# Gate and up products of a SwiGLU stage by seven block products instead of eight, on one Trainium2 core

## The chip, the cores and the metric

The kernel runs on 1 core of one Trainium2 chip. The core has a matrix engine (TensorE, PE in the profile; its weight loads are PEld), VectorE (DVE), ScalarE (ACT), GpSimd (POOL), a queue for transfers (SyncE, SP) and 16 DMA engines. The metric is the device time of one launch in microseconds; lower is better.

## The reference, cut to what matters

A decoder trunk of two layers on 512 tokens of 1024 features, all in float32. Each layer has a retention branch, an mLSTM branch, a gated merge with an output projection and a LayerNorm, and then the part that the change is about:

```python
gu = x @ w_gate_up[l]                                   # (512, 1024) @ (1024, 5632)
hidden = jax.nn.silu(gu[..., :D_FF]) * gu[..., D_FF:]   # D_FF = 2816
x = _layer_norm(DEEPNORM_ALPHA * x + hidden @ w_down[l], ln2_g[l], ln2_b[l])
```

## The kernel before, in words

**Products of split operands.** Every matrix product is made from operands split into a high part (rounded to the matrix engine's fast float32 format, `F32R`) and a low part (the rest). A product is the sum of three matmuls: high by high, high by low, low by high. The activations are held transposed, features on the 128 partitions, as a pair of tiles [128, 8 k-tiles, 512 tokens].

**The weight stream.** All weights lie in DRAM as units of [128, 1024] float32, in the order in which they are used (`layer_plan`, L48-90). An "F" unit holds 128 output columns for all 8 k-tiles; a "T" unit holds 512 columns of two k-tiles. For each unit SP issues a DMA of 512 KB into a raw tile (L133-139, `NRAW` = 3 raw tiles), ScalarE casts it to a high part `whi` (L147) and VectorE subtracts to make the low part `wlo` (L126, called from L154). `take` hands a prepared unit to the matmuls, `used` counts it off and prepares up to `LOOK` = 5 units ahead into a ring of `NRING` = 6 pairs. 

**Order of work.** The instructions of TensorE and SP stand in program order (`manual_schedule`, L100). Those of the other engines are placed by a scheduler of the framework, and each engine then works through its list in that order. Tiles with the same tag share a fixed number of buffers, and an instruction that writes a tile waits until the buffer's earlier tile is done with.

**Stages of a layer.** Retention, its gate and projection; mLSTM, its gate and projection; the output projection in two halves of 512 columns (`tok_units`, then `tok_blocks`, which holds four units over all four token blocks and ends each block with its LayerNorm, L722-738). `block_flip` (L740-751) transposes each normed block into the pair `x1h`, `x1l`: per half block one ScalarE cast (L750) and one VectorE subtraction.

**SwiGLU before.** For each of 22 tiles of 128 hidden features there is one gate unit and one up unit. Each is one `feat` (L194-199): 8 k-tiles times 3 matmuls of 128x128 weights by 512 tokens (L188-190) into one PSUM bank. The gate bank becomes SiLU on ScalarE (L816); the up bank is multiplied with it on VectorE (L824); the hidden tile is split at once, high on ScalarE (L825), low on VectorE (L126), into tiles that lie in buffers free by then. The first four units (hidden tiles 0 and 1) are done by `feat_split` (L214-224): the first 256 tokens of all four, between them the last two flips, then the other 256 tokens.

**Down stage before.** `tok_units` and `tok_blocks` over 22 hidden tiles, two per unit, twice (512 columns each, `DOWN0` and `DOWN1`, L44-45), with 128x128 blocks of the hidden tiles against 512 columns of weights (L247-249), and the residual and LayerNorm at the end.

Of the kernel before, what the change touches and what calls it, by code (L numbers as in the profile page):

```python
# [15 lines left out]
P = 128  # L16
# [14 lines left out]
# Columns of w_in.  # L31
# [13 lines left out]
DOWN1 = [(k, k + 1) for k in range(8, FT, 2)] + [(0, 1), (2, 3), (4, 5), (6, 7)]  # L45


def layer_plan():  # L48
    """Order of the weight units of a layer: ("F", matrix, column) holds 128 columns of all 8
    k-tiles, ("T", matrix, (k0, k1), column) holds 512 columns of two k-tiles."""  # L50
# [34 lines left out]
    for j in range(FT):  # L85
        feat("gu", j * P)
        feat("gu", DFF + j * P)
    tok("down", 0, DOWN0)
# [4 lines left out]
NUNIT = len(layer_plan())  # L93
UNIT_IF = layer_plan().index(("F", "if", 0))
# [3 lines left out]
def decoder_trunk(ctx: ExitStack, tc: tile.TileContext, wall, xT_in, x_in, pvec, lnp, rtab, out):  # L98
# [30 lines left out]
    total = L * NUNIT  # L129
    raw_t, prep_t = {}, {}  # L130
    state = {"dma": 0, "prep": 0, "used": 0, "next": 0}

    def issue_dma(n):  # L133
        while state["dma"] < min(n, total):
            i = state["dma"]
            r = wp.tile([P, UNIT], F32, tag="raw", name="wraw", bufs=NRAW)
            nc.sync.dma_start(r, wall[i])
            raw_t[i] = r
            state["dma"] += 1

    def prep_to(n):
        while state["prep"] < min(n, total, state["used"] + NRING):
            i = state["prep"]
            issue_dma(i + 1)
            r = raw_t.pop(i)
            hi = wp.tile([P, UNIT], F32R, tag="hi", name="whi")
            nc.scalar.copy(hi, r)  # L147
            lo = None
            if i % NUNIT == UNIT_IF:
# [51 lines left out]
    def feat_if(xh, xl, evac):  # L201
        """The gate columns are few: high parts in the first half of the columns, low ones in the second."""
# [11 lines left out]
    def feat_split(xh, xl, evacs, between):  # L214
        """The first units behind a norm: two token blocks first, the others when they are there."""
# [9 lines left out]

    def first_units(evacs):
        """The first units, in step with the loads of the activations."""
        ws = [take() for _ in evacs[:NRAW]]
# [11 lines left out]
        for ev in evacs[NRAW:]:  # L240
            feat(xh, xl, ev)
# [9 lines left out]
    def tok_units(pms, sh, sl, kts, first, last, evac=None):  # L251
        """Units of two k-tiles over all token blocks, one after the other."""
        for n, kk in enumerate(kts):
            w = take()
# [10 lines left out]
    def tok_blocks(pms, sh, sl, kts, first, evac, within):  # L265
        """Units of two k-tiles, one token block after the other."""
# [34 lines left out]
    for i in range(NRAW):  # L301
        firsts.append([wp.tile([P, UNIT], F32, tag="raw", name="wraw", bufs=NRAW),
                       wp.tile([P, UNIT], F32R, tag="hi", name="whi"), wp.tile([P, UNIT], F32R, tag="lo", name="wlo")])
# [18 lines left out]
    state["dma"] = state["prep"] = NRAW  # L322
    tab = reg.tile([P, 6, S], F32, tag="tab", name="rtab")
    nc.sync.dma_start(tab[:, 0:2], rtab[:, 0:2])
    issue_dma(NRAW + 1)
    nc.sync.dma_start(tab[:, 2:6], rtab[:, 2:6])
    issue_dma(2 * NRAW)
# [48 lines left out]
    def three(pa, a, b, first, last):  # L376
        """Product of two split operands without the product of their low parts."""
# [4 lines left out]
    def weighted(box, vh, vl, hh, nv, done):  # L382
        """Sums over s of weights and values, a token block at a time."""
# [59 lines left out]
    for l in range(L):  # L443
# [22 lines left out]
        # ---- mLSTM gates, by halves of the tokens: log sigmoid, its running sum b from the half's start,  # L466
        # a = i - b, M = max(m, running max a) with m the stabiliser at the half's start ----
# [254 lines left out]
        def block_norm(b, y, st, gb, dst):  # L722
            """LayerNorm of a token block."""
# [16 lines left out]
        def block_flip(b, y, nxt):  # L740
            """A token block transposed and split for the next products."""
            nh, nl = nxt
            for c in range(2):
# [7 lines left out]
                lo_of(nl[a], src, nh[a])  # L751

# [25 lines left out]
        ev0, ev1, within, between = norm_evacs(xr, gb, x1d, (x1h, x1l))  # L778
# [5 lines left out]
        hAh, hAl = bigpair(cur, f"h{l}")  # L784
        hid = {}
        for k in range(8):
            hid[k] = (hAh[:, k], hAl[:, k])

        def piece(tag, k0):
            t = reg.tile([P, 4, S], F32R, tag=tag, name=f"hd_{tag}")  # L790
            return t

        hp = {}

        def hidden(j):
            if j in hid:
                return hid[j]
            if j < 20:
                tags = {2: ("vh", "vl"), 3: ("gt", "qk"), 4: ("pp", "oo")}[j // 4]
                if tags not in hp:  # L800
                    hp[tags] = (piece(tags[0], j), piece(tags[1], j))
                a, c = hp[tags]
                hid[j] = (a[:, j % 4], c[:, j % 4])
            else:
                if "tab" not in hp:
                    hp["tab"] = piece("tab", j)
                a = hp["tab"]
                hid[j] = (a[:, (j - 20) * 2], a[:, (j - 20) * 2 + 1])
            return hid[j]
# [10 lines left out]
        def up_ev(j):  # L820
            def ev(pm):
                s = gates.pop(j)
                hh, hl = hidden(j)
                nc.vector.tensor_tensor(out=s, in0=s, in1=pm, op=ALU.mult)  # L824
                nc.scalar.copy(hh, s)  # L825
                lo_of(hl, s, hh)
            return ev

        feat_split(x1h, x1l, [gate_ev(0), up_ev(0), gate_ev(1), up_ev(1)], between)
        for j in range(2, FT):  # L830
            feat(x1h, x1l, gate_ev(j))
            feat(x1h, x1l, up_ev(j))

        xr = []
        for b in range(NB):
            t = scratch([P, DM], "xr2")
            nc.gpsimd.dma_start(t, x1d[b * P : (b + 1) * P, :])
            xr.append(t)
        hh_, hl_ = (lambda k: hid[k][0]), (lambda k: hid[k][1])
# [3 lines left out]
        else:  # L843
            nxt = bigpair(oth, f"x2{l}")
# [8 lines left out]
        tok_units([aux_bank() for _ in range(NB)], hh_, hl_, DOWN0, True, True, ev0)  # L853
        pms = [main_bank() for _ in range(NB)]
        tok_units(pms, hh_, hl_, DOWN1[:2], True, False)
        gb[0] = reg.tile([P, 2, DM], F32, tag="vh", name="gb2")
        nc.gpsimd.dma_start(gb[0], lnp[l, 2:4].unsqueeze(0).broadcast_to([P, 2, DM]))
        tok_units(pms, hh_, hl_, DOWN1[2:7], False, False)
        tok_blocks(pms, hh_, hl_, DOWN1[7:], False, ev1, within)
        if not last:  # L860
            xh, xl = nxt
# [5 lines left out]
def _layout(inputs):  # L867
# [32 lines left out]
    # Tables of the positions: rotary cosines and signed sines, decays of the four heads.  # L900
# [39 lines left out]
```

## Time and profile before

| what | value |
|---|---|
| time, median of 3 runs | 1830.61 us (1829.69 to 1831.13) |
| span of the profiled execution | 1828.3 us |
| the median over that span | 2.3 us more |
| instructions | 21351 |
| bytes moved by DMA | 200.71 MB, mean 110 GB/s |
| weight transfers from SP | 307 of 512 KB |
| mean granted TensorE clock | 0.997 of full speed |

The profiled execution is one of its own. Its time is given by its span, from the first to the last instruction; what lies around that is not in the profile. In the page, a row of a group ends with its busy time and the mean ns of one instruction, then the idle time of the engine before them and what ended it. Durations of matmuls overlap, so the rate of TensorE is read from the distance of their starts.

### The profile page before, as it was taken

The page shows a single profiled execution, that of the slowest core. Times are in us where ns is not written, and L with a number is a line of the kernel's source. Part 1 is how long each engine was busy: PE and PEld are TensorE (multiplying, and loading weights), DVE is VectorE, ACT ScalarE, POOL GpSimd, SP SyncE. Part 2 cuts the span into 40 slices and gives each one's busy share as a digit, 9 for nine tenths or more (in the row PEclk, how much of TensorE's full clock was granted, in tenths as well). Part 3 has the DMA queues.
Part 4 walks back from the last instruction along what each step waited for, and adds up shares of the span by engine and source line. Part 5 has one row for each costly group of instructions (what it writes and reads, how often), then busy time and mean ns, then how long its engine had stood idle before and what let it go on. Part 6 is the DMA issues. An engine that isn't in the chain of part 4 may idle for free.

```text
span 1828.3 us, 21351 instructions
## 1 busy us (share of the span) xinstructions
PE 1812.2 (99%) x8600; PEld 1518.3 (83%) x8600; DVE 874.2 (48%) x1406; ACT 644.4 (35%) x932; POOL 106.7 (6%) x145
## 2 busy tenths in 40 slices
PE   8999999999999999999999999999999999999998
PEld 7788888888889888888898888888888888888886
DVE  6665236654455333323476543467525643333234
ACT  4434326554313223221144343357432233222220
POOL 2020000010000000000120100010100100000000
PEclk9999999999999999999999999999999999999999
DMA  6222243234224232342432222422433332223321
GB/s 232 82 84 78 93 150 105 81 127 156 97 93 139 92 104 93 108 134 93 149 128 86 87 81 93 163 87 75 150 138 103 105 126 92 96 101 115 126 104 46
DMA packets 55011, 200.71 MB, mean 110 GB/s; under 512 B 6233, under 2 KB 8153, under 8 KB 52865
## 3 DMA queue, kind: packets, MB, share of 16 engines
q1 hardware_dynamic: 48528, 168.32, 27.5%
q0 software_dynamic: 6384, 31.04, 4.7%
q8 instruction: 67, 1.10, 0.3%
q14 instruction: 32, 0.25, 0.0%
HBM read 186.73 MB, written 12.60 MB: 109 GB/s over the span
## 4 chain that ended last, share of the span: by engine, by line
PE 96%; DVE 2%; ACT 1%; issue 1%; DMA 0%; SPq 0%; DVEq 0%; ACTq 0%
PE pm L190 18%; PE pm L188 18%; PE pm L189 18%; PE pm L247 9%; PE pm L249 9%; PE pm L248 9%; PE pa L248 3%; PE pa L247 3%; PE pa L249 3%; PE pa L378 1%; PE pa L379 1%; PE pa L380 1%; PE pa L433 1%; PE pa L352 1%; DVE wlo L126 1%
## 5 line engine op out<-in xcount | busy, mean ns | idle before, releaser
L126 DVE TENSOR_TENSOR wlo<-wraw,whi 128x1024 fp32r<-128x1024 f32 (+2 forms) x320 | 380.4, 1192 | 526.3 <-ACT whi L147 518.9
L147 ACT CAST whi<-wraw 128x1024 fp32r<-128x1024 f32 x307 | 322.9, 1052 | 859.8 <-PE pm L189 376.1
L188 PE MATMUL pm<-x11h,whi 128*128 128x512 f32 (+1 forms) x384 | 142.8, 372 | 0.0
L188 PE MATMUL pm<-x10h,whi 128*128 128x512 f32 (+1 forms) x384 | 142.8, 372 | 0.0
L189 PE MATMUL pm<-x10l,whi 128*128 128x512 f32 (+1 forms) x384 | 142.6, 371 | 0.0
L189 PE MATMUL pm<-x11l,whi 128*128 128x512 f32 (+1 forms) x384 | 142.6, 371 | 0.0
L190 PE MATMUL pm<-x10h,wlo 128*128 128x512 f32 (+1 forms) x384 | 142.6, 371 | 0.0
L190 PE MATMUL pm<-x11h,wlo 128*128 128x512 f32 (+1 forms) x384 | 142.6, 371 | 0.0
L188 PE MATMUL pm<-x20h,whi 128*128 128x512 f32 (+1 forms) x288 | 106.9, 371 | 0.0
L247 PE MATMUL pm<-whi,x0h 128*128 128x512 f32 x256 | 102.7, 401 | 3.3 <-DVE rvl L126 1.7
L190 PE MATMUL pm<-x20h,wlo 128*128 128x512 f32 (+1 forms) x288 | 105.4, 366 | 0.0
L189 PE MATMUL pm<-x20l,whi 128*128 128x512 f32 (+1 forms) x288 | 105.3, 366 | 0.0
L247 PE MATMUL pm<-whi,x20h 128*128 128x512 f32 x256 | 102.3, 400 | 0.6 <-DVE rvl L126 0.6
L249 PE MATMUL pm<-wlo,x0h 128*128 128x512 f32 x256 | 100.7, 393 | 0.0
L248 PE MATMUL pm<-whi,x0l 128*128 128x512 f32 x256 | 100.5, 393 | 0.0
L249 PE MATMUL pm<-wlo,x20h 128*128 128x512 f32 x256 | 100.3, 392 | 0.0
L248 PE MATMUL pm<-whi,x20l 128*128 128x512 f32 x256 | 100.0, 391 | 0.0
L824 DVE TENSOR_TENSOR sl<-sl,pm 128x512 f32<-128x512 f32 x44 | 30.3, 688 | 138.1 <-PE pm L190 138.1
L188 PE MATMUL pm<-x0h,whi 128*128 128x512 f32 x232 | 91.8, 396 | 0.0
L190 PE MATMUL pm<-x0h,wlo 128*128 128x512 f32 x232 | 90.4, 390 | 0.0
L189 PE MATMUL pm<-x0l,whi 128*128 128x512 f32 x232 | 90.3, 389 | 0.0
L188 PEld LDWEIGHTS pm<-x10h,whi 128*128 128x128 f32 x384 | 72.3, 188 | 12.6
(346 smaller groups left out, 3608.6 us busy)
## 6 DMA issues: line engine op xcount, KB each, us to landing
wraw<-wall SPq DMA_DIRECT2D x307, 512.0 KB, 3.3
yd<-sga POOLq DMA_DIRECT2D x4, 1024.0 KB, 5.0
ya<-yd POOLq DMA_DIRECT2D x4, 1024.0 KB, 6.1
gb<-lnp POOLq DMA_DIRECT2D x4, 1024.0 KB, 5.4
x1d<-xr POOLq DMA_DIRECT2D x8, 512.0 KB, 2.9
xr<-x1d POOLq DMA_DIRECT2D x8, 512.0 KB, 4.7
negm<-md POOLq DMA_DIRECT2D x2, 1026.0 KB, 6.7
xr<-xtok POOLq DMA_DIRECT2D x4, 512.0 KB, 3.9
```

What stands on the lines that cost most here:

```text
L126: nc.vector.tensor_tensor(out=out_lo, in0=full, in1=hi.bitcast(F32), op=ALU.subtract)
L147: nc.scalar.copy(hi, r)
L188: nc.tensor.matmul(pm[:, c0:c1], lhsT=hi[:, k], rhs=xh[:, k, c0:c1], start=(k == 0), stop=False)
L189: nc.tensor.matmul(pm[:, c0:c1], lhsT=hi[:, k], rhs=xl[:, k, c0:c1], start=False, stop=False)
L190: nc.tensor.matmul(pm[:, c0:c1], lhsT=lo[:, k], rhs=xh[:, k, c0:c1], start=False, stop=(k == KT - 1))
L247: nc.tensor.matmul(pm, lhsT=sh(k)[:, a], rhs=hi[:, j], start=first, stop=False)
L248: nc.tensor.matmul(pm, lhsT=sl(k)[:, a], rhs=hi[:, j], start=False, stop=False)
L249: nc.tensor.matmul(pm, lhsT=sh(k)[:, a], rhs=lo[:, j], start=False, stop=last)
L352: nc.tensor.matmul(pa[:, :HC], lhsT=k[:, t0:t1], rhs=q[:, t0:t2], start=True, stop=True)
L378: nc.tensor.matmul(pa, lhsT=a[0], rhs=b[0], start=first, stop=False)
L379: nc.tensor.matmul(pa, lhsT=a[0], rhs=b[1], start=False, stop=False)
L824: nc.vector.tensor_tensor(out=s, in0=s, in1=pm, op=ALU.mult)
```

## The change

The four units of two gate tiles and two up tiles are taken as one **quad**: a product of a 1024 x 512 weight matrix with 1024 x 512 activations. Both are seen as 2 x 2 blocks: the weights by halves of the k-tiles and by (gate pair, up pair), the activations by halves of the k-tiles and halves of the tokens. Seven block products in the manner of Strassen (Winograd's form) take the place of eight. It holds for hidden tiles 2 to 21, 10 quads a layer; tiles 0 and 1 stay as they were.

- **Weight operands.** Seven per quad in place of four units: blocks B11, B22, B21 as loaded, and T1 = B11 + B12, T3 = B22 + B12 (VectorE additions in place on the raw tile), T2 = T1 + B22 and T4 = T2 + B21 (DMAs issued by GpSimd that add a block from DRAM onto the raw tile). Each operand is then cast and split as a unit was.
- **Activation operands.** Four sums of x1 blocks, once per layer, from an unsplit copy `xf` that `block_flip` now also writes; each is cast and split.
- **Products.** Each is 2 x 4 x 3 = 24 matmuls of 128x128 weights by 256 tokens. Two products are added in PSUM to one before them (p2 onto p1, p4 onto p7).
- **Evacuation.** Copies and SiLU on ScalarE, four combinations on VectorE, two subtractions and two multiplications on GpSimd per quad.
- **Hidden tiles** 0 to 18 stay unsplit in float32 until the down stage, where `split_hidden` splits them up to six tiles ahead; tiles 19 to 21 are split at once.
- **Buffers.** The ring has 5 prepared pairs (`NRING`), look-ahead 4 (`LOOK`), 5 raw tiles (`NRAW`). The second down half goes through the hidden tiles in the same order as the first, and the gains for the last norm lie in another buffer.

```diff
-NRING = 6
-NRAW = 3
-LOOK = 5
+NRING = 5
+NRAW = 5
+NFIRST = 3
+LOOK = 4
-DOWN1 = [(k, k + 1) for k in range(8, FT, 2)] + [(0, 1), (2, 3), (4, 5), (6, 7)]
+DOWN1 = DOWN0
+QUAD_BLOCKS = ((0, 0), (1, 1), (0, 1), (1, 0))
+QUAD_OPS = ("B11", "B22", "T1", "T3", "T2", "B21", "T4")
...
+            if i in QUADS:
+                loads += [(m, kc) for kc in QUAD_BLOCKS]
+                operands += [(o, n) for o in QUAD_OPS]
+                ends[n + 1], ends[n + 2], ends[n + 3], ends[n] = (len(operands) - k for k in (4, 4, 2, 1))
...
+    def operand_of(kind, n):
+        need = {"B22": 1, "T1": 2, "B21": 3}.get(kind, 0)
+        issue_dma(n + need + 1)
+        f = raw_t[n]
+        if kind in ("B22", "B21"):
+            return raw_t[n + need]
+        if kind == "T1":
+            nc.vector.tensor_tensor(out=f, in0=f, in1=raw_t[n + 2], op=ALU.add)
+        elif kind == "T3":
+            f = raw_t[n + 1]
+            nc.vector.tensor_tensor(out=f, in0=f, in1=raw_t[n + 2], op=ALU.add)
+        elif kind in ("T2", "T4"):
+            nc.gpsimd.dma_start(pairs(f), block(loads[n][0], (1, 1) if kind == "T2" else (1, 0)), accum_op=ALU.add)
+        return f
...
-            issue_dma(i + NRAW)
+            while state["dma"] < len(loads) and ends.get(state["dma"] - NRAW, -1) < state["prep"]:
+                issue_dma(state["dma"] + 1)
...
+    def quad(xh, xl, sh, sl, ev):
+        t1, t2 = slice(0, S // 2), slice(S // 2, S)
+        banks = {n: main_bank() if n != "b" else aux_bank() for n in "aecdb"}
+        x1, x2 = slice(0, 4), slice(4, 8)
+        for name, act, bank, first in (("p1", (x1, t1), "a", True), ("p3", 3, "e", True), ("p5", 0, "c", True),
+                                       ("p7", 2, "d", True), ("p6", 1, "b", True), ("p2", (x2, t1), "a", False),
+                                       ("p4", (x2, t2), "d", False)):
+            w = take()
...
+            for j in range(2):
+                pm = banks[bank][:, j * 256 : (j + 1) * 256]
+                for k in range(4):
+                    go = first and j == 0 and k == 0
+                    for n, (x, y) in enumerate(((hi, ah), (hi, al), (lo, ah))):
+                        nc.tensor.matmul(pm, lhsT=x[:, j, k], rhs=y[:, k], start=go and n == 0,
+                                         stop=j == 1 and k == 3 and n == 2, skip_group_check=not first)
+                slot()
+            used()
+            ev(name, banks)
...
+                if xf is not None:
+                    nc.scalar.copy(xf[c][:, :, b * P : (b + 1) * P], src)
...
+        def sums():
...
+            for i, (a, b, op) in ((0, (a21, a22, ALU.subtract)), (1, (0, a11, ALU.subtract)),
+                                  (3, (1, a12, ALU.add)), (2, (a11, a21, ALU.subtract))):
+                f[i] = scratch([P, 4, S // 2], "sf")
+                nc.vector.tensor_tensor(out=f[i], in0=f[a] if isinstance(a, int) else a, in1=b, op=op)
+            for i in (3, 0, 2, 1):
+                nc.scalar.copy(sh[:, i], f[i])
+                lo_of(sl[:, i], f[i], sh[:, i])
...
+                if name == "p1":
+                    nc.scalar.copy(two("qa")[:, 0], banks["a"])
+                elif name == "p5":
+                    nc.scalar.copy(two("qa")[:, 1], banks["c"])
+                elif name == "p7":
+                    nc.vector.tensor_tensor(out=two("qb")[:, 1], in0=t["qa"][:, 1], in1=banks["d"], op=ALU.subtract)
+                elif name == "p6":
+                    u, v = t["qa"][:, 0], t["qa"][:, 1]
+                    nc.vector.tensor_tensor(out=u, in0=banks["b"], in1=u, op=ALU.add)
+                    nc.gpsimd.tensor_tensor(out=v, in0=v, in1=u, op=ALU.subtract)
+                    nc.vector.tensor_tensor(out=t["qb"][:, 0], in0=banks["e"], in1=v, op=ALU.add)
+                    nc.gpsimd.tensor_tensor(out=t["qb"][:, 1], in0=t["qb"][:, 1], in1=u, op=ALU.subtract)
+                elif name == "p2":
+                    nc.scalar.activation(two("qc")[:, 0], banks["a"], AF.Silu)
+                elif name == "p4":
+                    g = t["qc"]
+                    nc.vector.tensor_tensor(out=g[:, 1], in0=banks["d"], in1=t["qa"][:, 0], op=ALU.add)
+                    nc.scalar.activation(g[:, 1], g[:, 1], AF.Silu)
...
+                            nc.gpsimd.tensor_tensor(out=w, in0=up[:, i], in1=g[:, i], op=ALU.mult)
...
-        for j in range(2, FT):
-            feat(x1h, x1l, gate_ev(j))
-            feat(x1h, x1l, up_ev(j))
+        for j in range(2, FT, 2):
+            quad(x1h, x1l, sh, sl, quad_ev(j))
...
+        def split_hidden(n):
+            while place["next"] < min(n, NHF):
...
+                nc.scalar.copy(hh, w[:, i])
+                lo_of(hl, w[:, i], hh)
...
+        split_hidden(4)
...
-        tok_units([aux_bank() for _ in range(NB)], hh_, hl_, DOWN0, True, True, ev0)
+        tok_units([aux_bank() for _ in range(NB)], hh_, hl_, DOWN0, True, True, ev0, lambda k: split_hidden(k + 6))
```

More of the change, by code (lines that the diff above doesn't have):

```diff
@@ L93 @@
 NUNIT = len(layer_plan())
+QUADS = [layer_plan().index(("F", "gu", j * P)) for j in range(2, FT, 2)]
 UNIT_IF = layer_plan().index(("F", "if", 0))
@@ L781, in decoder_trunk @@
         tok_blocks([main_bank() for _ in range(NB)], mh, ml, K8, True, ev1, within)
[L784 to L793, printed above, removed]
-        def hidden(j):
[L796 to L809, printed above, removed]
+        NHF = 19
+        hf_t = {}
+        def hidden(j):
+            tag = ("vh", "vl", "gt", "oo", "qk")[j // 4]
+            if tag not in hf_t:
+                hf_t[tag] = reg.tile([P, 4, S], F32, tag=tag, name=f"hf_{tag}")
+            return hf_t[tag], j % 4
         gates = {}
```

128 lines of the change are left out of this document (101 added, 27 removed).

## The prediction

> **What bounds the kernel now.** The first view is the page: the span, the busy rows, the chain that ended last.
>
> ```profile
> span 1828.3 us, 21351 instructions
> PE 1812.2 (99%) x8600; PEld 1518.3 (83%) x8600; DVE 874.2 (48%) x1406; ACT 644.4 (35%) x932; POOL 106.7 (6%) x145
> PE 96%; DVE 2%; ACT 1%; issue 1%; DMA 0%; SPq 0%; DVEq 0%; ACTq 0%
> ```
>
> TensorE is busy 1812 of 1828 us and carries 96% of the chain; the rest is start, the gate scan of each layer and the tail. So time can come only from fewer TensorE cycles, and a change that makes TensorE wait pays at once. The median of the runs, 1830.61, is 2.3 us above this span; I add differences worked out on the span to that median.
>
> The second view is the windows over the two SwiGLU stages, the third the timeline of TensorE inside them (start, duration, instruction).
>
> ```profile
> 571.96:806.70 234.74, 234.74 (x1058) 195.29 (x1057) 81.94 (x89) 69.02 (x88) 2.13 (x4) 1.00 0.33 110
> 1476.30:1711.20 234.90, 234.90 (x1058) 195.38 (x1057) 82.10 (x89) 69.05 (x88) 2.13 (x4) 1.00 0.33 110
> 562.96 0.28 PE L188 MATMUL pm<-x10h,whi 128*128 128x256 f32 x1
> ...
> 571.96 0.28 PE L188 MATMUL pm<-x10h,whi 128*128 128x256 f32 x1
> 600.14 0.39 PE L188 MATMUL pm<-x10h,whi 128*128 128x512 f32 x1
> ...
> 608.30 0.39 PE L188 MATMUL pm<-x10h,whi 128*128 128x512 f32 x1
> ```
>
> The windows list, per stretch, the busy time of PE, PEld, DVE, ACT and POOL, the granted clock, the DMA share and GB/s. TensorE never waits there (234.74 of 234.74), the clock is 1.00, VectorE is busy a third, POOL not at all. In the timeline durations overlap; what counts is the distance of starts. Between the two 256-column rows lie 75 steps in 9.00 us: 120.0 ns each. Between the two 512-column rows lie 36 steps in 8.16 us: 226.7 ns each. Half the columns thus cost 53% of a full matmul, because of a fixed part of 13 ns.
>
> **The main term.** Four weight units cost 4 x 24 = 96 matmuls of 512 columns: 96 x 0.2267 = 21.76 us. A quad of the change costs 7 products x 24 matmuls of 256 columns, each a 128x128 weight block against 256 tokens as in the rows above: 168 x 0.1200 = 20.16 us, 2.88 us per product. There are 10 quads per layer: 20 x (20.16 - 21.76) = -32.0 us. The arithmetic falls by an eighth (2.72 us a quad); the fixed part of the shorter matmuls takes 1.12 of that.
>
> The Trainium skill, "TensorE: Matmul & The Clock Gate", section Back-to-back issue gap, gives a warm gap of columns / 2.4 + 2.5 ns. By it (an estimate) the gaps would be 109.2 and 215.8 ns and the term -47 us; the rows above differ from it at both sizes, and the measurement decides.
>
> **The other engines in a quad.** All other work must fit below 20.16 us, in order, on time.
>
> ```profile
> L126 DVE TENSOR_TENSOR wlo<-wraw,whi x320: 284/1226/1818, 5.0 to 1788.4; 128x1024 fp32r<-128x1024 f32 x152, 128x256 fp32r<-128x256 f32 x5, 128x128 fp32r<-128x128 f32 x3
> L147 ACT CAST whi<-wraw x307: 1033/1053/1063, 22.5 to 1787.3; 128x1024 fp32r<-128x1024 f32 x154
> L816 ACT ACTIVATE sl<-pm x44: 587/587/598, 570.8 to 1694.5; 128x512 f32<-128x512 f32 x44
> L824 DVE TENSOR_TENSOR sl<-sl,pm x44: 687/689/689, 571.5 to 1699.3; 128x512 f32<-128x512 f32 x44
> L825 ACT CAST h0h<-sl x8: 614/622/623, 572.3 to 643.3; 128x512 fp32r<-128x512 f32 x8
> L126 DVE TENSOR_TENSOR h0l<-sl,h0h x8: 684/685/686, 573.6 to 644.5; 128x512 fp32r<-128x512 f32 x8
> L459 POOL TENSOR_TENSOR rqk<-rqk,rt x16: 1291/2318/2336, 28.2 to 1027.5; 128x512 f32<-128x512 f32 x16
> ```
>
> These are rows per tile (minimum/median/maximum ns). VectorE gets 7 low parts and the sums T1 and T3, 9 x 1.23, and four combinations from PSUM, 4 x 0.69: 13.8 us. ScalarE gets 7 casts x 1.05 and four copies and SiLUs x 0.59: 9.7 us. POOL gets four operations on 512 elements: 4 x 2.32 = 9.3 us, and issues two DMAs. No sum reaches 20.16, so none becomes the bound by its total. Removed per quad: four products and splits of hidden tiles, which lay beside TensorE and cost nothing; the splits return in the down stage.
>
> The Trainium skill, "GPSIMD Engine Reference", section 3.1, has GpSimd at about 2.6 cycles an element on such an operation, an estimate of 1.1 us. The 2.32 us of the row is twice that; by the page POOL would need 4.4 us a quad and the pacing term below would be nil.
>
> **The accumulating DMAs.** T2 and T4 are made by a DMA from POOL that adds a weight block onto the raw tile. No such DMA is in the trace. The nearest rows (issues, KB each, median us to landing):
>
> ```profile
> wraw<-wall SPq DMA_DIRECT2D x307, 512.0 KB, 3.3
> ya<-yd POOLq DMA_DIRECT2D x4, 1024.0 KB, 6.1
> x1d<-xr POOLq DMA_DIRECT2D x8, 512.0 KB, 2.9
> xr<-x1d POOLq DMA_DIRECT2D x8, 512.0 KB, 4.7
> rtab<-rtab POOLq DMA_DIRECT2D x1, 1536.0 KB, 7.6
> POOL xr L837 <- DVE hd_oo L126: 428.9, 4, 204.1
> ```
>
> It moves 512 KB but must read the tile it adds to as well. Bounds: 2.9 us, as a plain store, and 7.6 us, as three times the bytes; I take 5.0, a little above the plain load of 4.7, and call it A. The last row (a wait: total, times, longest) shows a DMA at the head of POOL's queue holding that queue for up to 204 us; here that harms no one, but in the change arithmetic stands in the same queue.
>
> Now the due times, from a quad's start, with the next quad's operands primed. T1' can be cast when the high buffer of the fifth product is free, at 5 x 2.88 = 14.4 us: 1.05 + 1.23 end at 16.9 with hops. POOL's two subtractions behind the fifth product run from 15.4 (after one 0.69 combination) for 4.6, to 20.0. T2's DMA issues at 20.1, lands at 20.1 + A = 25.1, is split by 27.4. If T4's DMA issues then, it lands at 32.5, is split by 34.8, and is due when the fourteenth product starts, 13 x 2.88 = 37.4: slack 2.6, so no wait up to A = 6.3. But T2's cast ends at 26.2; if the SiLU of the seventh product stands behind that cast on ScalarE, and T4's DMA behind the two POOL multiplications that need this SiLU, then 26.2 + 0.6 + 0.1 + 4.6 puts the issue at 31.5, the landing at 36.5, the split at 38.8: 1.4 late. A wait w before that product delays the next quad as well, so w settles at half: 0.7 + (A - 5) us per quad. Which order holds is decided by a scheduler that places by readiness, not by the program:
>
> ```profile
> 609.93 0.69 DVE L824 TENSOR_TENSOR sl<-sl,pm 128x512 f32<-128x512 f32 x1 [3.38 <-PE pm L190]
> 610.77 1.23 DVE L126 TENSOR_TENSOR wlo<-wraw,whi 128x1024 fp32r<-128x1024 f32 x1
> ```
>
> L824 belongs to the evacuation, which the program writes after the weight's split; it overtook it. I take half of 0.7: 0.35 x 20 = +7 us, bounds 0 and +66 (A = 7.6 in the bad order: 3.3 x 20).
>
> The same freedom decides the raw tiles: five live tiles cover four blocks and one ahead. The raw tile of T4 is free last; if the next quad's loads take the two tiles free after T3, as I assume, they land well before use.
>
> **Entry, ring and down stage.** Before the first quad four sums of the activations come in: 4 x 1.23 of additions and 4 x 1.23 of low parts on VectorE, 9.8 us; on ScalarE four casts and eight copies of 0.59. From 562.4 to 580 VectorE is idle before these groups:
>
> ```profile
> L126 DVE TENSOR_TENSOR wlo<-wraw,whi 128x1024 fp32r<-128x1024 f32 x4 | 4.9, 1226 | 6.8 <-ACT whi L147 6.8
> L824 DVE TENSOR_TENSOR sl<-sl,pm 128x512 f32<-128x512 f32 x2 | 1.4, 688 | 1.5 <-PE pm L190 1.5
> L126 DVE TENSOR_TENSOR x10l<-pa,x10h 128x512 fp32r<-128x512 f32 x2 | 1.3, 686 | 1.4 <-ACT x10h L750 1.4
> ```
>
> 9.7 us idle against 9.8 wanted, with T1 and T3 on top, but three sums are due only with the third to fifth product. +1.5 a layer, +3 (0 to +20).
>
> The ring of prepared units falls from six to five. Where four units are held by a block-ordered stage (three such places before a norm's consumers), one spare is left instead of two: at worst one cast and split, 2.3 us, each. TensorE's own waits in the middle of the kernel are these, all for PSUM evacuations behind VectorE:
>
> ```profile
> PE pm L247 <- DVE rvl L126: 2.3, 2, 1.7
> PE pm L247 <- DVE rows L478: 1.2, 1, 1.2
> ```
>
> None is for a weight, so the look-ahead has room: +2 (0 to +7).
>
> In the down stage each unit (24 matmuls, 5.44 us) gets two splits of hidden tiles, 2 x 0.69 on VectorE beside its 1.23, 2 x 0.62 on ScalarE beside 1.05: hidden. At its start the first two must be split already. Their inputs exist since the first units, so by readiness they go early: +1 a layer, +2. In program order they would wait behind the last quad: 0.69 + 0.59 + 2 x 2.32 + 0.62 + 0.69 + 2 x 1.3 = 9.8 a layer, +20.
>
> **Sum:** -32 + 7 + 3 + 2 + 2 = -18 us: 1830.6 - 18 = 1812.6.
>
> **Rivals.** (1) *The accumulate chain paces the quads* (slower). The place is TensorE before the seventh product, the price w. For it: POOL's 2.32 us, its blocked queue, two DMAs in series. Against: the slack of 2.6 us in the good order. With 7 us of edges, 20 w must exceed 25: w = 1.25, so in the bad order A decides from 5.55 us up. At A = 6.1 (the 1 MB row) w is 1.8: -32 + 36 + 7 = +11, 1841.6; at 7.6, +41, 1871.6. Middle: about 1856. (2) *Clean*: the chain keeps up and the edges are covered: -32, 1798.6. For it: the idle VectorE; against: three queues exactly in time. (3) *The edges eat it*: half the sums uncovered (+10), splits in program order (+20), -32 + 30 = -2, 1828.6, from 1820 to 1836. For it: VectorE's full entry; against: L824's overtaking. (4) *It is not an eighth less*: matmuls paced by their weight load:
>
> ```profile
> L188 PEld LDWEIGHTS pm<-x10h,whi x384: 187/188/192, 552.0 to 793.7; 128*128 128x128 f32 x192
> ```
>
> 168 x 0.188 = 31.6 us a quad, +197, 2027. The 120.0 ns rows speak against it: loads of 188 ns follow each other there at 120.
>
> **How the numbers follow.** Chances: forecast 0.47, rival 1 0.26, rival 2 0.15, rival 3 0.11, rival 4 0.01. 0.2% is 3.7 us, about what a measurement of this kernel can tell from no change. Faster: 0.47 + 0.15 + 0.04 of rival 3 = 0.66; same: 0.06 of rival 3; slower: 0.26 + 0.01 + 0.01 = 0.28. The range starts at 1797, rival 2 less the runs' scatter of about 1.5, and ends at 1852, which holds nearly half of rival 1; out remain about 0.15 above and 0.04 below. The likeliest case's own range is 1800 to 1826.
>
> **What would show it.** Right: 256-column rows 120 ns apart through the stage, 20.2 to 20.9 us per quad, each SwiGLU stage's quads about 201.6 to 209 us where now 217.6 (40 x 5.44), accumulates landing in about 5 us. Waits of TensorE on the low part of T4 of over 1.25 us per quad would show rival 1; a wait at the first down unit or before the second product of the first quad, rival 3. The forecast is wrong if accumulates take over 6.3 us, or if loads wait for T4's raw tile, which would put load, sums and both accumulates into one loop.

## The result, and the profile after

The changed kernel takes 2000.70 us (median of 4 runs, 2000.11 to 2002.10); the kernel before, in the same comparison, 1830.53 (1829.69 to 1831.13). The ratio is 1.0931, with a 95% interval of 1.0915 to 1.0946: slower by 170 us, where 18 us less were forecast and the range ended at 1852. Two later kernels with seven products and no adding DMA, one of them complete and one that leaves out the making of T2 and T4, stand at 1794 us: without the adding DMAs the change was worth 36 us, and the way in which two of its operands are made cost 206. The 1794.4 us of the complete one is the median of three runs; a fourth took 2189.6 us at a mean granted clock of 0.752 and is left out of it.

The page of the changed kernel: span, busy rows, granted clock in 40 slices, chain.

```profile
span 1999.1 us, 24887 instructions
PE 1827.5 (91%) x10040; PEld 1603.1 (80%) x10040; DVE 1048.8 (52%) x1562; ACT 737.6 (37%) x1056; POOL 296.7 (15%) x265
PEclk9999999999999888799999999999999888888999
PE 7%; DMA 5%; issue 3%; DVE 2%; POOL 1%; ACT 1%; DVEq 0%; ACTq 0%; POOLq 0%
```

No engine is full: TensorE, at 99% before, now idles 9% of the span, and VectorE, ScalarE and GpSimd are about half busy or less. The clock row dips in two places, the two SwiGLU stages. The chain could be followed back over only a part of the span, so the waits answer the question instead. TensorE's own waits, most costly first (total us, times, longest):

```profile
PE pm L303 <- DVE qb L931: 150.9, 20, 9.5
PE pm L303 <- ACT qa L927: 2.9, 2, 1.6
PE pa L303 <- DVE wlo L137: 2.6, 4, 0.8
```

One wait per quad, 7.5 us each. L303 is the quad's matmul; L931 is the VectorE instruction that takes the seventh product p7 (fourth in the order of work) out of its PSUM bank d. The last product, p4, is added in PSUM onto p7's bank only once the bank is read, so TensorE stops before p4. The windows over the quads of each layer, then, in layer 0, the first row of the SwiGLU stage, the first of the quads, two wait rows one quad apart and two rows behind the second wait:

```profile
572.91:876.35 303.44, 224.27 (x1682) 221.27 (x1681) 143.12 (x135) 96.09 (x120) 89.57 (x59) 0.85 0.45 109
1563.16:1869.90 306.74, 228.25 (x1683) 225.27 (x1682) 143.22 (x135) 96.20 (x121) 89.78 (x59) 0.85 0.44 107
```

```profile
548.15 0.28 PE L245 MATMUL pm<-x10h,whi 128*128 128x256 f32 x1
...
572.91 0.28 PE L303 MATMUL pm<-x10h,whi 128*128 128x256 f32 x1
...
657.80 0.58 PE L303 MATMUL pm<-x10h,whi 128*128 128x256 f32 x1 [7.32 <-DVE qb L931]
...
688.14 0.58 PE L303 MATMUL pm<-x10h,whi 128*128 128x256 f32 x1 [8.27 <-DVE qb L931]
...
689.59 0.41 PE L303 MATMUL pm<-x10h,whi 128*128 128x256 f32 x1
689.81 0.41 PE L303 MATMUL pm<-x10l,whi 128*128 128x256 f32 x1
```

Quads take 303.44 + 306.74 = 610.2 us where the 40 units before took 2 x 217.6 = 435.2: 175 us more, a little over the whole loss of 170. A quad takes 30.34 us (657.80 to 688.14) against a forecast of 20.2 to 20.9. Of the 10.2 us over 20.16, about 7.5 are the wait; the rest is a slower clock: after each wait 256-column matmuls start 0.21 us apart, not 0.12, and the granted clock of the stage is 0.85. The stage starts at 548.15 (552.24 before) and its first four units take 24.8 us as before (572.91 - 548.15; 577.0 - 552.24), so neither start nor entry lost anything.

The adding DMAs, by the page's last part (KB each, median us to landing):

```profile
wraw<-wall POOLq DMA_DIRECT2D x40, 512.0 KB, 6.7
```

**The loop.** Timelines of one period: GpSimd, then ScalarE, then VectorE (start, duration; in brackets the idle time before and what ended it).

```profile
664.22 1.18 POOL L194 DMA_DIRECT2D wraw<-wall  x1
672.41 3.96 POOL L949 TENSOR_TENSOR hf_vl<-qb,qc 128x512 f32<-128x512 f32 x2 [7.00 <-ACT qc L943]
676.31 1.20 POOL L194 DMA_DIRECT2D wraw<-wall  x1
691.24 2.12 POOL L935 TENSOR_TENSOR qa<-qa 128x512 f32<-128x512 f32 x1 [13.73 <-DVE qa L934]
693.33 1.28 POOL L937 TENSOR_TENSOR qb<-qb,qa 128x512 f32<-128x512 f32 x1
694.56 1.18 POOL L194 DMA_DIRECT2D wraw<-wall  x1
```

```profile
670.67 1.05 ACT L203 CAST whi<-wraw 128x1024 fp32r<-128x1024 f32 x1 [8.88 <-DMA wraw<-wall]
671.63 0.63 ACT L943 ACTIVATE qc<-qc 128x512 f32<-128x512 f32 x1
...
682.80 1.99 ACT L203 CAST whi<-wraw 128x1024 fp32r<-128x1024 f32 x2 [9.13 <-DMA wraw<-wall]
684.69 0.58 ACT L929 COPY qa<-pm 128x512 f32<-128x512 f32 x1
```

```profile
683.87 2.36 DVE L137 TENSOR_TENSOR wlo<-wraw,whi 128x1024 fp32r<-128x1024 f32 x2 [8.66 <-ACT whi L203]
686.27 1.22 DVE L189 TENSOR_TENSOR wraw<-wraw 128x1024 f32<-128x1024 f32 x1
687.41 0.68 DVE L931 TENSOR_TENSOR qb<-qa,pm 128x512 f32<-128x512 f32 x1
...
690.40 0.68 DVE L934 TENSOR_TENSOR qa<-pa,qa 128x512 f32<-128x512 f32 x1
```

Read across the three. GpSimd issues T2's DMA at 664.22; ScalarE sits 8.88 us before it can cast T2 at 670.67. The SiLU of the earlier quad (L943) stands behind that cast (its input was there from 665.97 on), GpSimd's multiplications (L949) behind the SiLU, T4's DMA behind them: 676.31. ScalarE sits 9.13 us again, until T4 is there at 682.80. Behind T4's cast stands p5's copy (L929); behind T4's low part on VectorE stand the next sum T1 (L189), p7's evacuation (L931, for which TensorE waits) and p6's (L934). Behind that one stand GpSimd's subtractions, and behind them the next T2: 694.56, 30.34 us after the first. The evacuation of p7 can't overtake: it subtracts p7 from p5's copy, which ScalarE had not made before 684.69. The circle is closed. Of its 30.34 us the two landings up to the casts take 6.45 + 6.49 = 12.9; the other 17.4 are SiLU, multiplications, splits, sums and subtractions, which wait their turn in in-order queues while TensorE waits for them.

### The profile page after: what moved, and what is told of

Same layout as the page of the kernel before. It is cut to its first block, busy times and chain, and to the rows that moved or that the text cites. A ratio compares the mean times of both kernels' runs of the same rounds, so it can differ in the third digit from the quotient of the medians.

```text
span 1999.1 us, 24887 instructions
## 1 busy us (share of the span) xinstructions
PE 1827.5 (91%) x10040; PEld 1603.1 (80%) x10040; DVE 1048.8 (52%) x1562; ACT 737.6 (37%) x1056; POOL 296.7 (15%) x265
## 5 line engine op out<-in xcount | busy, mean ns | idle before, releaser
L137 DVE TENSOR_TENSOR wlo<-wraw,whi 128x1024 fp32r<-128x1024 f32 (+2 forms) x380 | 469.2, 1244 | 627.6 <-ACT whi L203 625.9
L203 ACT CAST whi<-wraw 128x1024 fp32r<-128x1024 f32 x367 | 381.9, 1049 | 893.3 <-DMA wraw<-wall 323.5
L303 PE MATMUL pm<-x11h,whi 128*128 128x256 f32 x240 | 80.3, 335 | 77.3 <-DVE qb L931 75.7
L303 PE MATMUL pm<-x10h,whi 128*128 128x256 f32 x240 | 78.5, 327 | 76.5 <-DVE qb L931 75.2
L420 POOL TENSOR_TENSOR rs<-ve,nhalf 128x4 f32<-128x4 f32 (+1 forms) x32 | 32.2, 1005 | 642.7 <-DVE ve L419 642.7
L303 PEld LDWEIGHTS pm<-x11h,whi 128*128 128x128 f32 x240 | 57.2, 238 | 79.5 <-DVE qb L931 64.9
L303 PEld LDWEIGHTS pm<-x10h,whi 128*128 128x128 f32 x240 | 55.3, 230 | 78.7 <-DVE qb L931 64.8
L935 POOL TENSOR_TENSOR qa<-qa 128x512 f32<-128x512 f32 x20 | 42.5, 2123 | 273.0 <-DVE qa L934 196.8
L303 PE MATMUL pm<-x11l,whi 128*128 128x256 f32 x240 | 78.2, 326 | 0.0
L303 PE MATMUL pm<-x11h,wlo 128*128 128x256 f32 x240 | 77.8, 324 | 0.0
```

The costliest lines, as they stand in the source:

```text
L137: nc.vector.tensor_tensor(out=out_lo, in0=full, in1=hi.bitcast(F32), op=ALU.subtract)
L303: nc.tensor.matmul(pm, lhsT=x[:, j, k], rhs=y[:, k], start=go and n == 0, stop=j == 1 and k == 3 and n == 2, skip_group_check=not first)
L420: nc.gpsimd.tensor_tensor(out=rs[:, :n], in0=ve[:, :n], in1=nhalf[:, :n], op=ALU.pow)
L935: nc.gpsimd.tensor_tensor(out=v, in0=v, in1=u, op=ALU.subtract)
```

## The experiments

Two theories were put against each other. **The loop:** queue order ties two adding DMAs and three engines into a circle of 30 us; it goes if the order is broken. **The latency:** two adding DMAs in series, with what goes with them, set the pace in any order. A third, that the place of the evacuations alone is at fault, would keep the loss where the DMAs are gone and the order stays. Unless a row says otherwise, the kernel before ran at 1829.9 to 1830.5 beside them.

**1 and 2. The DMAs away, the schedule left to the scheduler.** In the first, VectorE makes T2 and T4 by additions:

```diff
-            nc.gpsimd.dma_start(pairs(f), block(loads[n][0], (1, 1) if kind == "T2" else (1, 0)), accum_op=ALU.add)
+            nc.vector.tensor_tensor(out=f, in0=f, in1=raw_t[n + (1 if kind == "T2" else 3)], op=ALU.add)
```

with T3 kept in B12's tile, so that B22 and B21 live until they are used. In the second the DMA line is simply left out: T1's tile is cast and split again in the place of T2 and T4, so that the products are other ones, but their number and all instructions except the DMAs stay.

> T2 and T4 are made by VectorE additions (T3 is kept in the tile of B12, so that B22 stays for T2); no accumulating DMA is left. Theory L (a loop through two accumulating DMAs and three engine queues paces the quads at 30.3 us): the loop is gone, VectorE does 16.3 us of work per quad of 20.2 us, TensorE sets the pace: about 20.2 to 20.9 us per quad, 1795 to 1812 us in all. Rival W (the order of the evacuations on ScalarE and VectorE makes TensorE wait, with or without the DMAs): still a wait before the seventh product in each quad, 24 us or more per quad, over 1870 us.

> T2 and T4 are left out: the raw tile of T1 is cast and split again for both, no DMA and no addition. All other instructions stand. Theory L: the loop is gone and VectorE has 13.8 us per quad; TensorE runs through, 20.2 us per quad, 1790 to 1800 us. This is the price of everything but the making of T2 and T4. Rival W: over 1850 us.

Measured: 1794.4 us (three runs, 1794.3 to 1795.7; ratio 0.9805, interval 0.9785 to 0.9824) and 1794.2 (one run). Both times lie within 1 us of the loop's forecasts. Page and windows of the first, then the busy row of the second:

```profile
span 1792.5 us, 24827 instructions
PE 1778.1 (99%) x10040; PEld 1559.9 (87%) x10040; DVE 1117.8 (62%) x1602; ACT 743.5 (41%) x1056; POOL 253.4 (14%) x225
```

```profile
573.31:774.91 201.60, 201.60 (x1683) 201.60 (x1681) 178.21 (x156) 98.39 (x120) 68.34 (x39) 1.00 0.33 112
```

```profile
PE 1777.9 (99%) x10040; PEld 1559.4 (87%) x10040; DVE 1052.3 (59%) x1562; ACT 744.5 (42%) x1056; POOL 239.8 (13%) x225
```

Ten quads in 201.60 us are 20.16 each, the main term to the last digit, with TensorE busy all of it. VectorE does 40 operations more (x1602 against x1562), and with them is busy 178 of 201.6 us, 88%, but in time; the 40 additions take 1.85 us each at the mean (1.2 to 2.2). This version beats both kernels. The place of the evacuations alone is not at fault: the second kernel has the same program but for the two DMAs, and TensorE never waits in its quads. Nor did the scheduler find it a better order. In the middle quads of a layer ScalarE and VectorE work through the same lines of the program in the same order in the changed kernel, in the second kernel here, and in the one with plain DMAs below. So it takes both, the order and the landings, to close the circle.

**3 and 4. One link of the circle at a time.** The DMA kept but overwriting instead of adding (`accum_op` removed, which leaves out the sums in T2 and T4); and all four GpSimd operations of a quad moved to VectorE (`nc.gpsimd.tensor_tensor` becomes `nc.vector.tensor_tensor` on four lines).

> The two DMAs of a quad from GpSimd overwrite the raw tile with the weight block and do not add, so T2 and T4 are other operands. Theory L: only the landing time falls, from 6.7 us to the 4.5 us of the plain 512 KB loads from GpSimd; twice that per quad, 30.3 to about 26 us, 1910 to 1930 us in all. Rival A (the adding itself is what is slow, queue order does not matter): the slowdown goes, 1795 to 1830 us. Rival W: 2000 us as before.

> The four arithmetic operations of a quad that stood on GpSimd are on VectorE; GpSimd only issues the two accumulating DMAs. Theory L: two multiplications (4.0 us) and two subtractions (3.4 us) leave the loop, some 1.4 us come in on VectorE: about 24 us per quad, 1870 to 1900 us. Rival A: the two DMAs are unchanged, 30 us per quad, 2000 us.

Measured: 1897.71 and 1965.48 us (one run each). In each kernel's waits and DMA issues (KB each, us to landing), the plain DMA first:

```profile
PE pm L303 <- DVE qb L931: 70.1, 18, 6.0
```

```profile
wraw<-wall POOLq DMA_DIRECT2D x40, 512.0 KB, 4.2
```

```profile
PE pm L303 <- DVE qb L931: 117.2, 20, 7.4
```

```profile
wraw<-wall POOLq DMA_DIRECT2D x40, 512.0 KB, 7.6
```

The plain DMA lands in 4.2 us where the adding one took 6.7. 40 DMAs of 2.5 us less are 100 us, their shorter issue (0.74 for 1.20 us) 18 more; the time fell by 103. So in the circle nearly every microsecond of landing counts (the loop had forecast 1910 to 1930), but with the landings of a plain transfer the kernel still loses 103 us to the clean form. The second expectation failed: without GpSimd's arithmetic only 35 us came back, not 100 to 130. Its GpSimd queue, which now holds nothing but the DMAs in the quads, shows why:

```profile
661.15 1.17 POOL L194 DMA_DIRECT2D wraw<-wall  x1 [17.74 <-DVE wlo L137]
671.31 1.18 POOL L194 DMA_DIRECT2D wraw<-wall  x1 [8.99 <-DVE wlo L137]
690.23 1.18 POOL L194 DMA_DIRECT2D wraw<-wall  x1 [17.74 <-DVE wlo L137]
```

A second circle lies under the first. T2's DMA (661.15) must wait for T1's low part and T4's (671.31) for T2's, since each adds onto the tile that is being split; and T1's sum, cast and low part stand behind T4's cast and low part. From one T2 to the next this circle takes 29.08 us. The landings up to the casts took 7.56 and 8.78 us in it, 3.4 more than in the first. Taking away the longest branch of a loop brings only what the next branch leaves.

**5. The ring alone**, in the kernel before (`NRING` 5, `LOOK` 4, `NRAW` 5, `NFIRST` 3 on its loops):

> The kernel before with the change's buffers alone: 5 prepared pairs, look-ahead 4, 5 raw tiles. The prediction's term was +2 us (0 to +7). After the result, theory R: the SwiGLU stage began 4 us earlier with the new buffers, because more raw tiles are loaded ahead or the scheduler's order became a better one, so 1825 to 1828 us. Rival: those 4 us come from elsewhere in the change, and this run is 1830 to 1833 us.

Measured: 1829.0 us (11 runs, 1824.8 to 1829.3), ratio 0.9988 (0.9979 to 0.9997). The median is in neither expected range. In its trace, of a run of 1824.8 us, the SwiGLU stage starts at 547.03 where before 552.24: the buffers together save some us early in the kernel in that run. Which of them does is not shown; a cost of the shorter ring does not show.

**6. One adding DMA** (T2), T4 by VectorE, the scheduler's order:

> T4 is made by VectorE, T2 still by the accumulating DMA. Theory L: of the loop's 30.3 us one DMA (6.4 us) and the two multiplications ahead of its issue (4.0 us) go, one addition (1.2 us) comes: 21 us, close to TensorE's 20.2; 1795 to 1830 us. Rival A, by which each DMA costs in proportion: half of the loss stays, about 25 us per quad, 1890 to 1900 us.

Measured: 1871.97 us (one run), between the two expected ranges and in neither. ScalarE in one quad:

```profile
643.67 0.59 ACT L941 ACTIVATE qc<-pm 128x512 f32<-128x512 f32 x1
653.10 1.05 ACT L205 CAST whi<-wraw 128x1024 fp32r<-128x1024 f32 x1 [8.83 <-DMA wraw<-wall]
654.05 0.62 ACT L945 ACTIVATE qc<-qc 128x512 f32<-128x512 f32 x1
```

ScalarE stands still for 8.8 us behind a cast whose DMA has not landed, with the SiLU behind it: half the circle, and a quad of 23.8 us.

**7. The queues ordered by hand, both adding DMAs kept, nothing left out.** ScalarE, VectorE and GpSimd follow the program's order in the quads (`tc.manual_schedule`), and the program says after which product each operand is prepared; T2's and T4's DMAs are issued right behind the split of T1 and T2. First order:

> Both accumulating DMAs are kept, and every operation of the quads. The instructions of ScalarE, VectorE and GpSimd in the quads stand in a written order: evacuations ahead of the cast and the split of T4, T2's DMA right behind T1's split and ahead of the second subtraction, T1 prepared one product earlier. Theory L (the order in the in-order queues closes the loop): T4 is split by about 35.6 us on the clock of the prediction, due at 37.4; about 20.2 to 21.5 us per quad, 1795 to 1822 us. Rival A (two accumulating DMAs in series take too long in any order): 27 us or more per quad, over 1930 us.

Measured: 1927.45 us (ratio 1.0534, 1.0520 to 1.0549), 73 us better and not clean: far from the loop's forecast and all but at the latency's. ScalarE in it:

```profile
675.34 2.94 ACT L204 CAST whi<-wraw 128x1024 fp32r<-128x1024 f32 x3 [8.48 <-DMA wraw<-wall]
```

Three casts in a row after 8.48 us of waiting (T4's and two more): my order had put the next quad's first two operands behind T4. The second order puts them ahead of it, the third also casts T1 and issues T2's DMA ahead of T4's cast:

```diff
-        todo = {"p1": 6, "p7": 9, "p6": 10, "p2": 11, "p4": 12}
+        todo = {"p1": (4, 5), "p3": (7,), "p5": (8,), "p6": (6, 9), "p2": (10,)}
...
-        todo = {"p1": (4, 5), "p3": (7,), "p5": (8,), "p6": (6, 9), "p2": (10,)}
+        todo = {"p1": (4, 5), "p3": (7,), "p5": (8,), "p7": (9,), "p6": (6,), "p2": (10,)}
```

(The numbers are operands of the quad, 0 to 6 in the order of work, 6 being T4; 7 to 10 are the next quad's first four, 9 being its T1. In the first line a number says up to which operand, itself not included, all are prepared; in the others the operands are named one by one. The second and third order also change when the next weight loads are issued.)

> The changed kernel with both accumulating DMAs kept and nothing left out of the computation; only the order of the queues of ScalarE, VectorE and GpSimd in the quads is written by hand, in a second way. In the first hand-written order the next quad's first two operands still stood behind T4's cast, and ScalarE sat idle 7.0 to 8.5 us for T4's DMA in each quad (timeline). Now the next quad's B11 and B22 are cast behind the third and fifth evacuations, ahead of T4; T1 of the next quad is summed behind the seventh product's evacuation and its DMA for T2 is issued before the quad ends; T4 is cast behind p6's combination. The closed-loop theory (queue order makes the loop): from T2's issue at about 17.2 us of a quad 6.4 landing, 2.4 cast and split, 7 to 7.7 second landing, 2.4 split end at 35.4 to 36.1, before the last product of the next quad at 37.4, so TensorE waits little or not at all and the quads return to 20.2 to 20.8 us: 1795 to 1808 us. The rival that the latency of two DMAs in series paces in any order: no better than the first hand-written order, 1900 to 1930 us.

> The second hand-written order with both accumulating DMAs took 1864.57 us, 22.4 us a quad; its timeline still shows a loop: T4's landing, T4's cast, behind it T1's cast, T1's low part, T2's issue (664.6), T2's landing 7.6 later, split, T4's issue 11.2 us after T2's, landing 7.4 later. One edit: the next quad's T1 is cast and split, and T2's DMA issued, behind the seventh product's evacuation (the fourth in order), ahead of T4's cast instead of behind it. Nothing left out. Closed-loop theory: T2 then issues at about 15 us of a quad, T4 is landed 18.6 to 19 later and split by 36.5, due at 37.4: waits under 1 us a quad, 1795 to 1815 us. Rival (two landings of 7 to 8 us in series pace, or slow everything beside them): 1850 to 1870 us.

Measured: 1864.57 (1.0193, 1.0177 to 1.0208) and 1856.11 (1.0152, 1.0135 to 1.0169). Order thus takes the loss from 206 to 62 us over the clean form, with both DMAs in place. But neither kernel reached the loop's range, and the second lies in the range of the latency, 1850 to 1870. So order is worth some 145 of the 206, and what the 62 are is a question of its own (8). Adding DMAs landed in 7.6 and 7.4 us (medians) in these orders, more than in the circle.

**8. What is left in the last order.** TensorE waits there 12 times for a low part, up to 4.1 us. TensorE, GpSimd and VectorE around one such wait:

```profile
641.26 0.58 PE L316 MATMUL pm<-x10h,wlo 128*128 128x256 f32 x1 [3.50 <-DVE wlo L138]
```

```profile
637.18 1.73 POOL L953 TENSOR_TENSOR qa<-qa 128x512 f32<-128x512 f32 x1
638.41 1.71 POOL L957 TENSOR_TENSOR qb<-qb,qa 128x512 f32<-128x512 f32 x1
```

```profile
637.15 4.06 DVE L138 TENSOR_TENSOR wlo<-wraw,whi 128x1024 fp32r<-128x1024 f32 x1 [0.45 <-ACT whi L206]
```

T4's low part, 1.23 us elsewhere, takes 4.06: it ends at 641.21, 1.1 us after GpSimd's second subtraction ended at 640.12. Four more low parts of this layer do the same, with 2.6 to 4.1 us, and each ends 1.1 us after the subtraction. Two kernels take that apart: the subtractions moved to VectorE, DMAs kept (`nc.gpsimd` becomes `nc.vector` on two lines); and the DMAs left out, order and arithmetic kept.

> The order with T1 first and both accumulating DMAs (1856.11 us), with GpSimd's two subtractions per quad done by VectorE at the same place (0.7 to 1.3 us each); the two multiplications stay on GpSimd; nothing left out. In the trace of that order a low part of 1.22 us took 4.06 us on VectorE beside the two subtractions and T2's DMA issue, and TensorE waited 3.5 us for it in 12 of 20 quads. If this stretching is what is left: the long waits of 3 to 4 us on the low part go and the time falls by 25 to 45 us, to 1810 to 1830. If the landings pace: within 10 us of 1856.

> The order with T1 first and both accumulating DMAs (1856.11 us), with the two DMAs left out: T2 and T4 are then splits of T1's raw tile again, so the outputs are not the reference's; order, casts, splits and GpSimd's arithmetic are unchanged. If landings in series cost the last 61 us: 1794 to 1802 us. If the order itself does: 1835 us or more.

Measured: 1834.61 us (10 runs; ratio 1.0025, 1.0016 to 1.0035) and 1803.77 (0.9852, 0.9838 to 0.9867), 2 us above the first of its expected ranges. Moving the subtractions gives 21.5 us, a little less than the 25 forecast at the least; the long waits on the low part are gone. The waits of that kernel:

```profile
PE pm L316 <- DVE wlo L138: 15.2, 20, 0.8
PE pm L316 <- ACT whi L206: 11.2, 5, 3.6
```

Leaving the DMAs out (and with them the sums in T2 and T4) gives 52.3 us of the 61.7 left over the clean form, so the order that I wrote costs some 9 by itself. The 52 hold the 21.5 of the stretching; some 31 are the landings and what else goes with them. That split depends on the order in which the parts are taken away.

**9. One adding DMA in an order by hand**, T4 behind p6's evacuation, then one step earlier behind p7's, then no adding DMA at all:

> The same hand-written order with T4 made by VectorE and only T2 by an accumulating DMA, nothing left out. In the scheduler's order this pair of choices gave 1871.97 us, with ScalarE idle 7.5 us a quad behind the one DMA. Closed-loop theory: no wait of TensorE left, 1794 to 1800 us. Rival (the DMA's latency itself): 1850 to 1875 us. If this one is clean and the one with two DMAs is not, the second DMA in series is what does not fit in a period of 20.2 us.

> The hand-written order with one accumulating DMA, whose quads still took 21.8 us against 20.16: there T4's sum stood behind the combination of p6, and its cast and low part ended 0.4 and 0.8 us after the last product could start. One edit: T4 is summed, cast and split behind the seventh product's evacuation (the fourth in order) instead, 2.9 us earlier. Nothing left out. Closed-loop theory: no wait of TensorE left in the quads, 1794 to 1802 us. Rival (the DMA's latency, or the transfers beside it, slow the stage whatever the order): no change from 1841, at most 10 us.

> The last hand-written order with one accumulating DMA (1845.12 us), with that DMA replaced too: T2 is now a VectorE addition in front of its cast, and T3 is kept in the tile of B12 so that B22 stays for it. Nothing left out, no accumulating DMA. If the accumulating DMA is what still costs there: 1795 to 1805 us. If it is the order that I wrote: 1835 to 1850 us, no better than with the DMA; VectorE has one addition more (1.23 us a quad) in the same place.

Measured: 1841.01 (1.0060, 1.0043 to 1.0077), 1845.12 (1.0087, 1.0072 to 1.0102) and 1823.06 us (0.9964, 0.9950 to 0.9978). The first and the third missed both expectations; the second came out as the rival had it, with no gain from the earlier T4. The third shows part of the reason: the order of the second, with nothing to land, costs 29 us over the clean form, and its one DMA 22 on top. In the second kernel p7's evacuation stood behind four low parts on VectorE:

```profile
650.10 5.74 DVE L138 TENSOR_TENSOR wlo<-wraw,whi 128x1024 fp32r<-128x1024 f32 x4 [2.12 <-ACT whi L206]
655.77 0.67 DVE L951 TENSOR_TENSOR qb<-qa,pm 128x512 f32<-128x512 f32 x1
656.37 1.21 DVE L192 TENSOR_TENSOR wraw<-wraw 128x1024 f32<-128x1024 f32 x1
657.50 1.21 DVE L197 TENSOR_TENSOR wraw<-wraw 128x1024 f32<-128x1024 f32 x1
```

T4's sum (L197) thus gained nothing: it starts 2.4 us before p4 in both kernels (656.37 and 658.79 in the first, 634.93 and 637.35 in the second). An order that keeps both DMAs and runs clean was not found in these tries; that there is one is not shown, nor that there is none.

Taken together, the times came in where the loop had them only when both DMAs were gone in the scheduler's order (1 and 2); with DMAs left, no kernel did. What shows the circle are the queues in the traces, that the same order without landings runs clean, and that other orders with the same two landings take 73 to 145 us off.

## Why the prediction was wrong, step by step

- **Main term, -32.0: right.** Without the adding DMAs the quads take 20.16 us each, 201.60 per layer.
- **Other engines in a quad: totals right, use wrong.** VectorE needs 143 us in 303, and even with all additions 178 in 201.6. No total became a bound. GpSimd's four operations took 7.4 us a quad (2.12 + 1.28 + 3.96), less than the 9.3 of the sum. What the totals leave out is that a VectorE operation can be held up beside GpSimd's (4.06 us for 1.23).
- **Entry, +3: wrong by its size, 0.** The first four units take 24.8 us before and after. **Ring, +2: -1** at the median of the kernel with the buffers alone, up to -5 in its profiled run. **Down stage, +2: 0.** From the last quad to the next layer's first matmul it takes 999.4 - 876.35 = 123.1 us in the changed kernel and 917.63 - 794.62 = 123.0 before.
- **The accumulating DMAs, +7: the step that failed; it measures +206** against the clean form. Not for A: 6.7 us lies inside the bounds 2.9 to 7.6, above the 5.0 taken. Put into the prediction's own bad order, 0.7 + (6.7 - 5) = 2.4 us per quad give 48 and a total of 1853.6, still 147 us short. What failed is the due times. They hung each quad's chain on TensorE's clock: subtractions "from 15.4", T2 "at 20.1", "with the next quad's operands primed". That holds only if evacuations run on time. The prediction asked what stands behind T2's cast (the SiLU, and it found the bad order); it did not ask the same of T4's cast. Behind it the scheduler had placed p5's copy, T1's sum, p7's and p6's evacuations, and so the next quad's T2. With that the chain no longer has a slack to use up: it is a circle of 30.34 us, and its full length is the period.
- **Rival 1 had the place but not the price.** TensorE stops before the last product, as it said, but for p7's evacuation rather than T4's low part, and 7.5 us, not 1.25 to 3.3. The test named at the end, accumulates over 6.3 us, came true; the other, loads that wait for T4's tile, was the right kind of danger on another queue: in the quads of layer 0 ScalarE waited 20 times for a transfer, each time for an adding DMA and never for a load.
- **A cost nobody listed: the clock.** Of the 206 us about 49 are TensorE working slower after its waits (busy 1827.5 against 1778.1 in the clean form, with as many matmuls).
- **What stays open:** how the last 31 us in the third hand-written order divide between the latency of two landings and transfers that slow each other; the landing alone was not measured with nothing beside it.

## What to carry to other kernels

When an operation with a long latency feeds an in-order queue, list for each engine what stands behind its consumer, and follow every such item until it reaches a TensorE instruction or comes back to the next issue of the same operation; if it comes back, the period can't be shorter than that circle, and neither a sum of busy times nor a slack at one due time shows it. Look for the next circle too before taking a link out. Before a transfer that adds, see whether an engine has room to add: here VectorE had room for two additions of 1.85 us a quad, and doing so was 206 us faster. The scheduler here kept one order in the middle quads whether the transfers were slow, quick or absent, so read the order of the queues, not the order of the program.

## What the runs showed of the hardware

- An adding DMA of 512 KB from GpSimd's queue lands in 6.7 us at the median (6.1 to 9.0), a plain one at the same place in 4.2 (4.0 to 6.2), and its issue holds GpSimd for 1.20 us against 0.74. In the other kernels here the adding one's median is 5.9 to 7.6.
- TensorE's rate after a wait: 0.213 us from start to start at 256 columns (17 steps from 688.53 to 692.15; 689.59 to 689.81 is one) where 0.120 is its rate in the unbroken stage. The fast rate is back 4.2 us after the restart at 688.14. The Trainium skill, "TensorE: Matmul & The Clock Gate", section Back-to-back issue gap, gives a cold gap of columns / 1.2 ns, 213 ns here as an estimate; the trace agrees. So an idle stretch of 7 to 8 us costs twice, once as such and once in the matmuls behind it.
- VectorE's low part beside GpSimd's two subtractions took 4.06 us and ended 1.1 us after them, as if it had only then begun. The Trainium skill, "SBUF — State Buffer", section SBUF: two separate sides, says that a VectorE operation with two SBUF inputs and a GpSimd operation that reads SBUF exclude each other for a whole instruction. The trace agrees by the ends: the VectorE operation waited through two GpSimd instructions in a row. The recorded starts lie 0.03 us apart, VectorE's first, so they don't show which came first. A combination with one operand in PSUM kept its 0.69 us beside a GpSimd subtraction (663.06 in the changed kernel).
